# A third pair with fourteen products in the first mixer, and weight sums made by accumulating transfers

## The chip, the cores and the metric

The kernel runs on one core of a Trainium2 chip. The metric is the device time of one execution in microseconds (us). The engines are named as the profile names them: PE multiplies matrices (PEld is its loading of weights, which overlaps it), DVE works element by element on vectors, ACT applies functions and copies, POOL is a general engine that also issues transfers of its own, SP issues most transfers. DMA is the 16 engines that move the data.

## The reference, cut to what matters

A trunk of two residual layers over 256 tokens of 2048 features, all in float32. Layer 0 has stick-breaking attention, layer 1 an attention over selected keys; each is followed by an MLP. The change touches the input projection of layer 0 alone: 256 tokens times a weight of 2048 x 6144.

```python
def stick_breaking_mixer(h, w_in, w_out):
    q, k, v = jnp.split(h @ w_in, 3, axis=-1)      # w_in: 2048 x 6144
    ...                                            # 16 heads of 128
    z = jnp.einsum('bqhd,bkhd->bhqk', q, k) * scale
    log_1mb = jnp.where(causal, jax.nn.log_sigmoid(-z), 0.0)
    tail = lax.cumsum(log_1mb, axis=3, reverse=True) - log_1mb
    a = jnp.where(causal, jnp.exp(jax.nn.log_sigmoid(z) + tail), 0.0)
    ...
    return o @ w_out

x = x + stick_breaking_mixer(rms_norm(x, norm_mix[0]), w_in_a[0], w_out_a[0])
```

## The kernel before

**Items.** The whole kernel is one list of *items*. An item is one block of weights, 256 input features by 512 output columns (512 KB), and the matmuls that use it. A block is loaded into one of six raw tiles (`wraw`, issued by SP), and *split* into two parts whose sum it is: ACT writes the rounded part `wh` (line 2023), DVE the rest `wl` (line 2024). Activations are kept split in the same way. A plain item makes 12 matmuls of 128 x 512: two halves of the tokens, two blocks of 128 features, and for each the parts `wh` with both parts of the activations and `wl` with one. There are four buffers each of `wh` and `wl`, so the split of an item waits for the matmuls of the item four before it.

**Order.** The list is written out by hand, and each engine runs its instructions in the order of the program. For item i the program first issues the split of item i+2 (`LEAD` is 2) and the loads some items further on, then the matmuls of i, and then the steps that are hung on i (`at(i, f)`): steps of the projection first, in the order in which they were hung there, then those of the attention. An instruction that waits holds up all behind it on its engine.

**The first mixer's input projection.** q0, k0 and v0 (512 columns each) are done as 24 plain items (0 to 23). Then come pairs of column groups with the group v1 in between: the first pair (q1 k1, from item 24), v1 (46 to 53), the second pair (q2 k2, from 54), the third pair (q3 k3, from 76) and the fourth (v2 v3). After that comes the output projection.

**Products.** In a pair, some of the work on two column blocks (G and H) is done by a scheme of Strassen's kind: two blocks of 256 features, two halves of the tokens and two column blocks would be eight block products; the scheme needs seven, s1 to s7, of 6 matmuls each, at the price of sums of activations (`sums`, made once) and of weights. A *set* covers two of the eight blocks of features; SEVEN says which: set a the blocks 0 and 2, set b 1 and 3. ROLES gives the order of a pair's items and after which of them its steps stand. The role "mixer" has one set: 12 plain items and 7 products, 19 items. The role "mixer2" has two sets: 8 plain items and 14 products, 22 items. Products of the same name in both sets are summed in PSUM.

**Weight sums.** The sums of weights are the sources of four of the products, which have no block of their own. X feeds s5, Z feeds s6 and later, changed in place, s4, and Y feeds s7. Y is loaded with a block of its own. The steps T1 to T4 make the sums, all on DVE, from the raw tiles of s1, s2 and s3. P1 (ACT), P6, P5 and P7 (DVE) gather the products in E, and `gather` adds the plain items' results.

**Attention in between.** The attention of two heads at a time runs between the items. STEPS gives for each pair of heads the items after which its nine steps stand: logits z (PE, then ACT's copy and abs), exp and ln (ACT), plus (DVE, then POOL's causal select of e, line 1515), sph (ACT), spl (DVE), the tails (PE), the a-step (DVE, then ACT's exp and POOL's select of a), the output (PE, ACT) and its low part (DVE).

**Elsewhere.** The pairs of the MLP and of the output projections follow a planner (`Plan`) and have sums of additions alone; in them T3 is an accumulating transfer from POOL's queue (line 980): it adds a block from DRAM onto a tile.

Of the kernel before, what the change touches and what calls it, by code (L numbers as in the profile page):

```python
# [13 lines left out]
OP = mybir.AluOpType  # L14
# [3 lines left out]
P = 128  # L18
# [33 lines left out]
INNER = {"a": (0, 1), "b": (2, 3)}  # L52
STEPS = ((37, 42, 42, 44, 45, 48, 50, 59, 59),
# [7 lines left out]
ATTENTION = ([("PE", 1.3), ("A", 1.5)], [("A", 1.5)], [("V", 0.9)], [("A", 0.75)], [("V", 0.85)],  # L61
             [("PE", 1.2)], [("V", 0.9), ("A", 0.75)], [("PE", 1.3), ("A", 0.55)], [("V", 0.6)])
ORDER_B = "s1a s1b s5a . . s5b s6a s6b . s7a s7b . s3a s3b s2a s4a s2b s4b G0 G1 G2 G3"
OUT_SUMS = (118, 119)
BIAS = 262
ROLES = {
    "mixer": ("G0 H0 s1 G1 s3 H1 G2 s6 H2 s5 G3 s7 H3 s2 G4 H4 s4 G5 H5", dict(
        T1a=1, T2a=3, T3a=5, T4a=11, P1=5, P6=7, P5=10, P7=11)),
    "mixer2": ("G0 H0 s1a s1b s3a s5a G1 H1 s6a s3b s5b G2 s6b s2b s2a H2 s4a s4b s7a s7b G3 H3", dict(
        T1a=1, T2a=4, T3a=5, T4a=13, T1b=3, T2b=8, T3b=11, T4b=13, P1=3, P6=12, P5=17, P7=19)),  # L70
}


# [278 lines left out]
def trunk(ctx, tc, x, x_t, gains_t, w_in_a, w_out_a, w_in_b, w_in_b_end, w_out_b, rel_bias, w_up, w_down, out):  # L352
# [12 lines left out]
    act, dve, pool, pe = nc.scalar, nc.vector, nc.gpsimd, nc.tensor  # L365
# [3 lines left out]
    keep = tc.keep_in_program_order  # L369
# [30 lines left out]
    room = tmp.tile([P, 2 * P], F32, name="junk", bufs=1)  # L400
# [194 lines left out]
    def block_of(w, r0, c0):  # L595
        return w[r0 // (KB * P), c0 // 512].rearrange("p (a c) -> p a c", a=KB)
# [75 lines left out]
    def sums(at, where, src, s, a, b, n=0):  # L672

        st = {}

        def whole():
            h = src()
            st["a"] = a().rearrange("p q (j s) -> p q j s", j=KB)
            hi, lo = (h[:, 0:4 * KB, i, :].rearrange("p (q j) s -> p q j s", q=2)[
                :, :, KB * n:KB * n + KB] for i in range(2))  # L680
            keep(dve.tensor_add(st["a"], hi.bitcast(F32), lo.bitcast(F32)))

        def four():
            a = st["a"]
            st["b"] = b()
            z = st["b"].rearrange("p (s j) e -> p s j e", s=4)
            (a11, a21), (a12, a22) = ((a[:, q, :, :P], a[:, q, :, P:]) for q in range(2))
            keep(dve.tensor_add(z[:, 0], a21, a22))
            keep(dve.tensor_sub(z[:, 1], z[:, 0], a11))
            keep(dve.tensor_sub(z[:, 2], a11, a21))  # L690
            keep(dve.tensor_sub(z[:, 3], a12, z[:, 1]))

        def high():
            keep(act.activation(s()[:, 0], st["b"], AF.Copy))

        def low():
            keep(dve.tensor_sub(s()[:, 1], st["b"], s()[:, 0].bitcast(F32)))

        for i, step in zip(where, (whole, four, high, low)):
            at(i, step)  # L700

    def seven_products(items, at, sec, w, r0, cols, left, role, S, last=False):
# [34 lines left out]
        products = {}  # L737
# [22 lines left out]
        def own(q, t):  # L760
            return lambda part, j: left()[:, KB * q + j, part, t * P:(t + 1) * P]

        def block(col, q):
            return block_of(w, r0 + KB * P * q, cols[col])

        def spot(pos):
            return base + pos

        def p1():
            keep(act.activation(sec["E"][:, 0], products["s1"], AF.Copy))  # L770

        def p6():
            keep(dve.tensor_add(sec["E"][:, 1], products["s6"], sec["E"][:, 0]))

        def p5():
            keep(dve.tensor_add(sec["E"][:, 2], products["s5"], sec["E"][:, 1]))

        def p7():
            E = sec["E"].rearrange("p (a b) e -> p a b e", a=2)
            keep(dve.tensor_add(E[:, :, 1],  # L780
                                products["s7"].unsqueeze(1).to_broadcast([P, 2, 512]),
                                sec["E"][:, 1:3]))

        def gather(col):
            E = sec["E"][:, 2 * col:2 * col + 2]
            keep(dve.tensor_add(E, accs.pop(keys[col]), E))
# [3 lines left out]
        def one_set(n):  # L790
            qa, qb = SEVEN[n]
            room = sec[n]

            def summed(i):
                return lambda part, j: S(n)[:, part, KB * i + j, :]

            def raw(name):
                return seven[name + n].raw

            def load_y():  # L800
                keep(nc.sync.dma_start(room["Y"], block(1, qa)))

            def t1():
                room["X"] = room["new X"]()
                keep(dve.tensor_sub(room["X"], room["Y"], raw("s1")))

            def t2():
                keep(dve.tensor_sub(room["Z"], raw("s3"), room["X"]))

            def t3():  # L810
                keep(dve.tensor_sub(room["Y"], raw("s3"), room["Y"]))

            def t4():
                keep(dve.tensor_sub(room["Z"], raw("s2"), room["Z"]))

            for name, lhs, src, *to in (
                    ("s1", own(qa, 0), block(0, qa)), ("s2", own(qb, 0), block(0, qb), (0, 0)),
                    ("s3", summed(3), block(1, qb), (1, 0)), ("s4", own(qb, 1), "Z", (0, 1)),
                    ("s5", summed(0), "X"), ("s6", summed(1), "Z"), ("s7", summed(2), "Y")):
                seven[name + n] = seventh(name + n, lhs, src, *to)  # L820
            items[max(base - 8, room.get("read", 0) + 1)].early.append(load_y)
            room["read"] = base + order.index("s7" + n) - LEAD
            for name, step in (("T1", t1), ("T2", t2), ("T3", t3), ("T4", t4)):
                at(spot(place[name + n]), step)
# [283 lines left out]
    class Pair:  # L1108
# [21 lines left out]
        def block(self, col, q):  # L1130
            return block_of(self.w, self.r0 + KB * P * q, self.cols[col])
# [261 lines left out]
    def mixer_a():  # L1393
# [3 lines left out]
        sec = {"a": {}, "b": {}}  # L1397
# [178 lines left out]
        def out_rooms(heads):  # L1576
# [21 lines left out]
            for hp, where in enumerate(STEPS):  # L1598
                for i, work in zip(where, ATTENTION):
                    weave.plan.busy[i] += work  # L1600
            weave.out_columns(
                w_out_a, lambda: heads, parts, lambda i: st["oT", i], dict(zip("ab", OUT_SUMS)), {},
                {"aX": STEPS[7][0], "aZ": STEPS[7][0], "bX": STEPS[7][7], "bZ": STEPS[7][7]}, ORDER, 32)
# [3 lines left out]
            group(*front[g], q)  # L1607
        for g in range(FRONT):
            single(*front[g], FRONT * (QB - 1) + g)
        roles = ["mixer2", "mixer2", "mixer", "mixer"]  # L1610
        for names in "q1 k1,v1,q2 k2,q3 k3,v2 v3".split(","):
            groups = [(name[0], int(name[1])) for name in names.split()]
            if len(groups) == 2:
# [368 lines left out]


    sections = [mixer_a(), mlp(0, 16), mixer_b(), mlp(1, None)]
    items = [it for sec in sections for it in sec[0]]
    first, sizes, plans = {}, {}, {}
# [134 lines left out]
```

## Time and profile before

| | |
|---|---|
| time, median of 3 runs | 1988.82 us (1988.48 to 1989.84) |
| span of the profiled execution (first to last instruction) | 1986.8 us |
| PE busy | 1980.4 us, 8834 matmuls |
| DVE busy | 1785.0 us |
| ACT busy | 1301.7 us |
| POOL busy | 91.7 us |
| DMA | 498.44 MB, of which 33.56 MB by accumulating transfers |

The profiled execution has no time of its own beside its span; its time is taken as the span and the 2.0 us by which the median of the runs is above it. Busy time is the time in which an engine has an instruction under way; for PE it includes a wait inside the pipeline, which shows as a greater distance between matmuls. In the timelines a row is a start, a duration, an engine, a line of the kernel, an operation, what it writes and reads, and a count; engines overlap the end of one instruction with the start of the next, so the distance of two starts is a little less than the duration.

### The profile page before, as it was taken

The page shows a single profiled execution, that of the slowest core. Times are in us where ns is not written, and L with a number is a line of the kernel's source. Part 1 is how long each engine was busy: PE and PEld are TensorE (multiplying, and loading weights), DVE is VectorE, ACT ScalarE, POOL GpSimd, SP SyncE. Part 2 cuts the span into 40 slices and gives each one's busy share as a digit, 9 for nine tenths or more (in the row PEclk, how much of TensorE's full clock was granted, in tenths as well). Part 3 has the DMA queues.
Part 4 walks back from the last instruction along what each step waited for, and adds up shares of the span by engine and source line. Part 5 has one row for each costly group of instructions (what it writes and reads, how often), then busy time and mean ns, then how long its engine had stood idle before and what let it go on. Part 6 is the DMA issues. An engine that isn't in the chain of part 4 may idle for free.

```text
span 1986.8 us, 25525 instructions
## 1 busy us (share of the span) xinstructions
PE 1980.4 (100%) x8834; PEld 1635.3 (82%) x8834; DVE 1785.0 (90%) x1973; ACT 1301.7 (66%) x1573; POOL 91.7 (5%) x135
## 2 busy tenths in 40 slices
PE   9999999999999999999999999999999999999999
PEld 7888888888888888888888788788888888888887
DVE  6879869899999999989995898889998998998996
ACT  6567666667676676766764566666767676776664
POOL 0000100000000000020000000000000000000000
PEclk9999999999999999999999999999999999999999
DMA  9776766889788977889887698578887888788784
GB/s 350 215 238 189 218 211 181 275 289 292 244 259 257 278 235 239 288 277 295 247 291 235 190 264 255 153 264 281 290 265 244 254 269 271 224 286 276 256 244 146
DMA packets 233441, 498.44 MB, mean 251 GB/s; under 512 B 88608, under 2 KB 121440, under 8 KB 233312
## 3 DMA queue, kind: packets, MB, share of 16 engines
q1 hardware_dynamic: 216048, 455.81, 68.8%
q0 software_dynamic: 9216, 33.56, 9.4%
q10 hardware_dynamic: 8048, 7.45, 1.1%
q8 instruction: 69, 1.13, 0.2%
q14 instruction: 60, 0.49, 0.1%
HBM read 459.46 MB, written 37.22 MB: 250 GB/s over the span
## 4 chain that ended last, share of the span: by engine, by line
PE 99%; DVE 0%; DMA 0%; issue 0%; ACT 0%; SPq 0%; DVEq 0%
PE acc L1169 39%; PE acc L1151 26%; PE acc L628 17%; PE acc L732 5%; PE aux L1151 4%; PE aux L751 2%; PE acc L751 1%; PE acc L619 1%; PE aux L1851 0%; PE acc L1494 0%; PE aux L1554 0%; PE acc L1739 0%; PE aux L1169 0%; PE acc L1704 0%; PE aux L1556 0%; PE acc L1496 0%
## 5 line engine op out<-in xcount | busy, mean ns | idle before, releaser
L2024 DVE TENSOR_TENSOR wl<-wraw,wh 128x1024 fp32r<-128x1024 f32 (+1 forms) x670 | 805.5, 1217 | 134.6 <-ACT wh L2023 121.9
L2023 ACT ACTIVATE wh<-wraw 128x1024 fp32r<-128x1024 f32 (+1 forms) x670 | 700.0, 1053 | 317.8 <-PE acc L1169 110.7
L1169 PE MATMUL acc<-wh,xT 128*128 128x512 f32 x1152 | 284.6, 389 | 0.0
L1169 PEld LDWEIGHTS acc<-wh,xT 128*128 128x128 f32 x1152 | 216.2, 188 | 45.2 <-ACT wh L2023 0.3
L1169 PE MATMUL acc<-wh,half 128*128 128x512 f32 x1004 | 248.2, 389 | 0.0
L1169 PEld LDWEIGHTS acc<-wh,half 128*128 128x128 f32 x1004 | 188.5, 188 | 39.1
L1151 PE MATMUL acc<-wh,half 128*128 128x512 f32 x720 | 192.4, 389 | 0.0
L628 PE MATMUL acc<-wh,xT 128*128 128x512 f32 x736 | 185.5, 392 | 0.0
L628 PEld LDWEIGHTS acc<-wh,xT 128*128 128x128 f32 x736 | 137.6, 188 | 30.0 <-issue 1.7
L1151 PEld LDWEIGHTS acc<-wh,half 128*128 128x128 f32 x720 | 135.2, 188 | 28.1
L1169 PE MATMUL acc<-wl,xT 128*128 128x512 f32 x576 | 154.0, 389 | 0.0
L1169 PE MATMUL acc<-wl,half 128*128 128x512 f32 x502 | 134.4, 389 | 0.0
L1169 PEld LDWEIGHTS acc<-wl,xT 128*128 128x128 f32 x576 | 108.1, 188 | 22.5
L1151 PE MATMUL acc<-wl,half 128*128 128x512 f32 x360 | 110.8, 389 | 0.0
L1169 PEld LDWEIGHTS acc<-wl,half 128*128 128x128 f32 x502 | 94.2, 188 | 19.5
L628 PE MATMUL acc<-wl,xT 128*128 128x512 f32 x368 | 99.2, 391 | 0.0
L2023 ACT ACTIVATE wh<-Zb 128x1024 fp32r<-128x1024 f32 x60 | 63.5, 1058 | 41.5 <-PE acc L1169 14.4
L1151 PE MATMUL acc<-wh,xT 128*128 128x512 f32 x336 | 89.8, 389 | 0.0
L628 PEld LDWEIGHTS acc<-wl,xT 128*128 128x128 f32 x368 | 68.9, 188 | 15.0 <-DVE wl L2024 0.3
L732 PE MATMUL acc<-wh,xT 128*128 128x512 f32 x320 | 79.7, 391 | 0.0
L1151 PEld LDWEIGHTS acc<-wl,half 128*128 128x128 f32 x360 | 67.6, 188 | 14.0
L2024 DVE TENSOR_TENSOR wl<-Za,wh 128x1024 fp32r<-128x1024 f32 x60 | 73.4, 1223 | 0.7 <-ACT wh L2023 0.6
(404 smaller groups left out, 3087.2 us busy)
## 6 DMA issues: line engine op xcount, KB each, us to landing
wraw<-in_w_up_dram SPq DMA_DIRECT2D x228, 512.0 KB, 5.4
wraw<-in_w_down_dram SPq DMA_DIRECT2D x224, 512.0 KB, 5.1
wraw<-in_w_in_a_dram SPq DMA_DIRECT2D x88, 512.0 KB, 4.9
wraw<-in_w_in_b_dram SPq DMA_DIRECT2D x64, 512.0 KB, 4.8
jx<-tu SPq DMA_DIRECT2D x44, 512.0 KB, 5.8
tu<-y SPq DMA_DIRECT2D x128, 128.0 KB, 3.6
wraw<-in_w_out_a_dram SPq DMA_DIRECT2D x30, 512.0 KB, 3.6
wraw<-in_w_out_b_dram SPq DMA_DIRECT2D x30, 512.0 KB, 4.4
```

Source lines behind the costliest of these rows:

```text
L619: pin(pe.matmul(accs[key][t], L[:, j, part, t * P:(t + 1) * P], wx[:, j, :], start=(j == 0 and n == 0), stop=False))
L628: (keep if alone else pin)(pe.matmul(acc[t], L[:, KB * q + j, part, t * P:(t + 1) * P], wx[:, j, :], start=a and q == 0, stop=z and q == Q ...
L732: keep(pe.matmul(acc[:, t, :], L[:, KB * qs[i] + j, part, t * P:(t + 1) * P], wx[:, j, :], start=a and i == 0, stop=z and i == end - (last ...
L751: keep(pe.matmul(p, lhs(part, j), wx[:, j, :], start=to is None and a and n == sets[0], stop=to is None and z and n == sets[-1]))
L1151: keep(pe.matmul(o, lhs(part, j), wx[:, j, :], start=a and opens, stop=z, skip_group_check=True))
L1169: keep(pe.matmul(acc[:, t, :], L[:, KB * q + j, part, t * P:(t + 1) * P], wx[:, j, :], start=a and i == 0 and not self.sets, stop=z, skip_ ...
L2023: order(act.activation(wh[:, a], raw[:, a], AF.Copy))
L2024: order(dve.tensor_sub(wl[:, a], raw[:, a], wh[:, a].bitcast(F32)))
```

## The change

The third pair takes the role "mixer2" instead of "mixer": two sets, 22 items instead of 19. Everything after it in the mixer stands three items later (STEPS, OUT_SUMS), and the steps of the attention that fall into the third pair are moved a little against its items. T3 and T4 become accumulating transfers issued from POOL's queue, in all four pairs; since a transfer can only add, the signs of the sums of activations, of T1 and T2 and of the gathering steps are turned so that all sums of weights are additions. T3 and T4 stand earlier in the pair (T3a after its third item instead of the sixth, T4a after the ninth instead of the 14th or 12th). P7 becomes two instructions of half the size.

```diff
-         (59, 61, 61, 65, 66, 79, 85, 97, 105),
-         (67, 73, 75, 79, 86, 89, 90, 107, 113),
-         (87, 88, 88, 90, 91, 104, 105, 117, 117),
-         (92, 95, 97, 103, 106, 109, 110, 121, 121),
+         (59, 61, 61, 65, 66, 80, 86, 100, 108),
+         (67, 73, 75, 80, 88, 91, 93, 110, 116),
+         (89, 90, 90, 93, 95, 107, 108, 120, 120),
+         (95, 98, 100, 106, 109, 112, 113, 124, 124),
...
-OUT_SUMS = (118, 119)
+OUT_SUMS = (121, 122)
...
     "mixer": ("G0 H0 s1 G1 s3 H1 G2 s6 H2 s5 G3 s7 H3 s2 G4 H4 s4 G5 H5", dict(
-        T1a=1, T2a=3, T3a=5, T4a=11, P1=5, P6=7, P5=10, P7=11)),
+        T1a=1, T2a=3, T3a=2, T4a=8, P1=5, P6=7, P5=10, P7=11)),
     "mixer2": ("G0 H0 s1a s1b s3a s5a G1 H1 s6a s3b s5b G2 s6b s2b s2a H2 s4a s4b s7a s7b G3 H3", dict(
-        T1a=1, T2a=4, T3a=5, T4a=13, T1b=3, T2b=8, T3b=11, T4b=13, P1=3, P6=12, P5=17, P7=19)),
+        T1a=1, T2a=4, T3a=2, T4a=8, T1b=3, T2b=8, T3b=4, T4b=11, P1=3, P6=12, P5=17, P7=19)),
...
-            keep(dve.tensor_add(z[:, 0], a21, a22))
+            keep(dve.tensor_sub(z[:, 0], a21, a22))
             keep(dve.tensor_sub(z[:, 1], z[:, 0], a11))
             keep(dve.tensor_sub(z[:, 2], a11, a21))
-            keep(dve.tensor_sub(z[:, 3], a12, z[:, 1]))
+            keep(dve.tensor_add(z[:, 3], a12, z[:, 1]))
...
         def p5():
-            keep(dve.tensor_add(sec["E"][:, 2], products["s5"], sec["E"][:, 1]))
+            keep(dve.tensor_sub(sec["E"][:, 2], products["s5"], sec["E"][:, 1]))
 
         def p7():
-            E = sec["E"].rearrange("p (a b) e -> p a b e", a=2)
-            keep(dve.tensor_add(E[:, :, 1],
-                                products["s7"].unsqueeze(1).to_broadcast([P, 2, 512]),
-                                sec["E"][:, 1:3]))
+            E = sec["E"]
+            keep(dve.tensor_sub(E[:, 3], E[:, 2], products["s7"]))
+            keep(dve.tensor_add(E[:, 1], products["s7"], E[:, 1]))
...
             def t1():
                 room["X"] = room["new X"]()
-                keep(dve.tensor_sub(room["X"], room["Y"], raw("s1")))
+                keep(dve.tensor_add(room["X"], room["Y"], raw("s1")))
 
             def t2():
-                keep(dve.tensor_sub(room["Z"], raw("s3"), room["X"]))
+                keep(dve.tensor_add(room["Z"], raw("s3"), room["X"]))
 
             def t3():
-                keep(dve.tensor_sub(room["Y"], raw("s3"), room["Y"]))
+                keep(pool.dma_start(room["Y"], block(1, qb), accum_op=OP.add))
 
             def t4():
-                keep(dve.tensor_sub(room["Z"], raw("s2"), room["Z"]))
+                keep(pool.dma_start(room["Z"], block(0, qb), accum_op=OP.add))
...
-        roles = ["mixer2", "mixer2", "mixer", "mixer"]
+        roles = ["mixer2", "mixer2", "mixer2", "mixer"]
```

4 rows, old and new, of the table STEPS are left out of this document.

## The prediction

> **What bounds the kernel now.** I read the head of the page, the chain that ended last, and then a table of stretches cut where the pairs of the first mixer's input projection begin (71.01, 137.25, 184.34 and 231.14 us; the third pair is the stretch from 184.34).
>
> ```profile
> span 1986.8 us, 25525 instructions
> PE 1980.4 (100%) x8834; PEld 1635.3 (82%) x8834; DVE 1785.0 (90%) x1973; ACT 1301.7 (66%) x1573; POOL 91.7 (5%) x135
> ...
> PE 99%; DVE 0%; DMA 0%; issue 0%; ACT 0%; SPq 0%; DVEq 0%
> ```
>
> ```profile
> core 0: us, PE busy (x) PEld busy (x) DVE busy (x) ACT busy (x) POOL busy (x), PEclk, DMA share, GB/s
> 71.01:114.40 43.39, 43.39 (x198) 36.11 (x196) 40.26 (x37) 28.73 (x32) 1.69 (x2) 1.00 0.72 222
> ...
> 137.25:184.34 47.09, 47.09 (x220) 39.47 (x218) 42.51 (x40) 33.58 (x40) 3.46 (x4) 1.00 0.61 208
> 184.34:231.14 46.80, 46.80 (x216) 39.03 (x214) 38.26 (x36) 28.55 (x34) 5.97 (x8) 1.00 0.72 218
> ```
>
> The chain is 99% PE, and in every pair PE is busy for the whole stretch at clock 1.00. So a matmul less is worth its full time, an operation of another engine taken away is worth nothing, and any new wait of PE is lost whole: nothing later catches it up. DVE is nearly as full (40.26 of 43.39, 42.51 of 47.09, 38.26 of 46.80 us), so its queue is where a new wait would come from.
>
> The profiled execution's span is 1986.8 us against a median of 1988.82 us, so 2.0 us lie around the span. I make the sum as a difference and put it on 1988.82.
>
> **The change, part by part.**
>
> *Products.* The next fence has PE's timeline in the third pair: start, us, engine, line, operation, count. A line of several matmuls is one item or half of one.
>
> ```profile
> 212.37 2.10 PE L732 MATMUL acc<-wh,xT 128*128 128x512 f32 x8
> ...
> 216.58 0.39 PE L1530 MATMUL acc<-sph,tri 128*128 128x512 f32 x1
> ...
> 217.51 2.00 PE L732 MATMUL acc<-wh,xT 128*128 128x512 f32 x8
> ...
> 220.26 1.98 PE L732 MATMUL acc<-wh,xT 128*128 128x512 f32 x8
> ...
> 222.98 1.07 PE L751 MATMUL acc<-wh,xT 128*128 128x512 f32 x4
> ...
> 224.34 0.59 PE L1494 MATMUL acc<-qk 128*128 128x256 f32 x2
> ...
> 225.56 2.10 PE L732 MATMUL acc<-wh,xT 128*128 128x512 f32 x8
> ```
>
> A plain item (12 matmuls) takes 222.98-220.26 = 2.72 us, a product (6) 224.34-222.98 = 1.36 us: 0.2267 us a matmul. The logits of a pair of heads take 225.56-224.34 = 1.22, the tails 217.51-216.58 = 0.93. The third pair goes from 12 plain items and 7 products (186 matmuls) to 8 and 14 (180): 6 x 0.2267 = **1.36 us less**.
>
> *Splits and sums on DVE and ACT.* Three more items are three more splits on ACT and on DVE. Sums on DVE fall from 24 (six sets of four) to 14 (seven of two), 10 x 1.14 us; P7 becomes two halves in each pair. Over the mixer DVE gets lighter; PE hides it before and after, so I cost all of it at nothing, except where the order makes PE wait. In the third pair alone DVE does not get lighter: two sums a set, two sets, makes four as before, with three splits more (3 x 1.14 us) in a stretch 1.36 us shorter.
>
> *The new wait, at the third pair's G3.* In the new order the four products s4a, s4b, s7a, s7b (items 92 to 95) stand in a row, and G3 is item 96. The new STEPS put the logits of heads 8 and 9 after item 89, their exp, ln and plus at 90, the tails of heads 6 and 7 after 91, and the a-step of heads 6 and 7 and sph of heads 8 and 9 at 93. The split of item i+2 is issued ahead of item i's matmuls, so G3's split stands on ACT behind that exp of a and sph; they stand behind the a-step on DVE, and that behind the splits of 93, 94 and 95 and P5. The rows that price this, ACT first, then DVE:
>
> ```profile
> 212.65 0.81 ACT L1499 ACTIVATE z<-acc 128x768 f32<-128x768 f32 x1 [2.87 <-PE acc L1496]
> 213.49 0.85 ACT L1500 ACTIVATE e<-z 128x768 f32<-128x768 f32 x1
> 214.24 1.05 ACT L2023 ACTIVATE wh<-wraw 128x1024 fp32r<-128x1024 f32 x1
> 215.19 0.83 ACT L1504 ACTIVATE e<-e 128x768 f32<-128x768 f32 x1
> 216.05 0.85 ACT L1505 ACTIVATE e<-e 128x768 f32<-128x768 f32 x1
> 216.80 1.04 ACT L2023 ACTIVATE wh<-wraw 128x1024 fp32r<-128x1024 f32 x1
> ...
> 221.34 0.85 ACT L1542 ACTIVATE a<-a 128x768 f32<-128x768 f32 x1 [2.55 <-DVE a L1540]
> 222.10 0.83 ACT L1520 ACTIVATE sph<-e 128x768 fp32r<-128x768 f32 x1
> 222.83 1.99 ACT L2023 ACTIVATE wh<-wraw 128x1024 fp32r<-128x1024 f32 x2
> ```
>
> ```profile
> 210.01 0.68 DVE L776 TENSOR_TENSOR oTc<-aux,oTc 128x512 f32<-128x512 f32 x1
> 210.61 0.95 DVE L1524 TENSOR_TENSOR spl<-e,sph 128x768 fp32r<-128x768 f32 x1
> ...
> 216.93 0.96 DVE L1509 SCALAR_TENSOR_TENSOR e<-z,e 128x768 f32<-128x768 f32 x1 [0.39 <-ACT e L1505]
> 217.88 1.23 DVE L2024 TENSOR_TENSOR wl<-wraw,wh 128x1024 fp32r<-128x1024 f32 x1
> 219.02 1.43 DVE L2024 TENSOR_TENSOR wl<-oTc,wh 128x1024 fp32r<-128x1024 f32 x1
> 220.37 0.94 DVE L1540 TENSOR_TENSOR a<-z,acc 128x768 f32<-128x768 f32 x1
> ```
>
> Let T be the end of the logits after item 89. PE then has s2a 1.36, H2 2.72, the tails 0.93, four products 5.44 and the next logits 1.22: it comes to G3 at T+11.67. ACT: z's copy at T+0.28 (212.65-212.37), abs 0.84 later, split 92 0.75 later, exp 0.95 later, ln 0.86 later at T+3.68; ln ends at T+4.53, and split 93 may start at T+4.43. DVE: plus at T+4.56 (0.03 after ln, as at 216.93), free again 0.95 later, T+5.51. Three splits of 1.14 (219.02-217.88) reach T+8.93, P5 (0.60) T+9.53, the a-step ends 0.94 later at T+10.47. ACT: exp of a at T+10.50, sph 0.76 later, G3's split 0.73 later at T+11.99, done 1.04 later at T+13.03. PE waits 13.03-11.67 = **1.36 us**. What keeps this hidden now is that only two products stand between the plain items there. Its ends: 0 (if DVE is two splits earlier than laid out) and 2.0 (if P5 or the plus comes half a microsecond later). I take 1.36. Elsewhere the same laying out leaves 0.3 us or more.
>
> *The accumulating transfers.* T3 and T4 of all seven sets go to POOL's queue: 14 more, of 512 KB. The rows of those that stand in the kernel already: the queue's share, issue to landing by target, all together, and one group's time on POOL.
>
> ```profile
> q0 software_dynamic: 9216, 33.56, 9.4%
> ```
>
> ```profile
> qk<-in_w_out_a_dram POOLq DMA_DIRECT2D x1, 512.0 KB, 8.8
> Yb<-in_w_out_a_dram POOLq DMA_DIRECT2D x1, 512.0 KB, 8.0
> ```
>
> ```profile
> L980 POOL DMA_DIRECT2D Ya<-in_w_up_dram x14: 862/862/888, 403.1 to 1764.5; - x14
> ...
> DMA to landing us min/median/max: 5.5/8.6/10.8
> ```
>
> T3 has 7 items or more until its sum is split, and T4 of set a has 6, 8 us at the least of the items' own time: I cost both at nothing, covered by the products and plain items between. T4b has least: issued after item 11 of the pair, its sum split for item 17. It waits for DVE's split of s6b, and in the third pair also for the select of heads 4 and 5 (item 86), which stands ahead of it in POOL's queue.
>
> ```profile
> 207.95 0.77 POOL L1515 TENSOR_SCALAR_AFFINE_SELECT a<-a 128x256 f32<-128x256 f32 x2 [21.03 <-ACT a L1542]
> ...
> 218.02 2.69 POOL L1515 TENSOR_SCALAR_AFFINE_SELECT e<-e 128x256 f32<-128x256 f32 x2 [9.30 <-DVE e L1509]
> ```
>
> ```profile
> 161.93 1.21 DVE L2024 TENSOR_TENSOR wl<-vsb,wh 128x1024 fp32r<-128x1024 f32 x1
> ```
>
> ```profile
> 163.97 1.07 PE L751 MATMUL aux<-wh,oTb 128*128 128x512 f32 x4
> ```
>
> In the second pair that split ends (163.14) 0.83 us before its item starts (163.97). With T3a's sum (1.14) gone from DVE's queue I take 2.0 before. Then a-step 0.94, exp 0.88, select 0.77: T4b is issued 0.6 us after s6b starts, and since s6b, s2b and the logits take 3.94 us, at T-3.3. Its sum is wanted at T+4.43, so there are 7.7 us, and what the landing takes beyond that adds to the chain above one for one. Ends: 5.5 us, nothing; 10.8 us, 3.1. I take 8.0, the row of the same room in the same mixer: **0.3 us**. In the first two pairs no a-step, exp and select stand ahead, 2.6 us, so there are some 10 us and only landings past 10 cost there: 0.8 each at 10.8.
>
> The Trainium skill, "DMA: Bandwidth & Descriptors", section on the anatomy of a transfer issued by GpSimd, fits its time as 2.0 us plus the bytes over 436 GB/s, by my estimate 3.2 us for 512 KB; with it this term would be 0 and the sum 1988.8. The rows above (5.5 at least) do not agree.
>
> *DMA load.* 9.4% of 1986.8 us over 64 transfers is 2.92 us of all 16 engines each. The third pair has 0.72 x 46.80 = 33.7 us now; with four more, 45.4 of 45.4 us. The weight loads land in 4.4 us (the next row is of that stretch), and six raw tiles let them be issued several items ahead, so I cost this at nothing; but it is why an accumulate may land late. SP's queue gets no more transfers: 15 blocks and one Y become 14 and two.
>
> ```profile
> wraw<-in_w_in_a_dram SPq DMA_DIRECT2D x15, 512.0 KB, 4.4
> ```
>
> *Sum:* -1.36 + 1.36 + 0.3 = +0.3: **1989.1 us**.
>
> **The rivals.**
>
> 1. *All hidden.* G3 comes in time, T4b too: 1988.82-1.36 = 1987.5. For it: PE waits nowhere in the pairs now. Against: the chain above, which is short only if DVE runs over a microsecond earlier.
>
> 2. *T4b held at POOL.* The select ahead of it takes 2.69 instead of 0.77 us, as the selects of e do beside DVE: T4b 1.9 later, 2.2 us late in all, 1988.82-1.36+1.36+2.2 = 1991.0. Against: the row of the select of a. (The Trainium skill, "SBUF — State Buffer", section "Who interferes with whom", says that a DVE instruction with two SBUF inputs contends with a GpSimd instruction that reads SBUF, which speaks against the change; the two rows agree in kind, without saying which select is hit.)
>
> 3. *Slower: accumulates late from full DMA engines.* Place: the split of s4b, worst in the third pair. At 10.8 us it costs 3.1 there and 0.8 in each of the first two pairs: 1988.82-1.36+1.36+4.7 = 1993.5. It passes 0.2% at a landing of 10.6 us, where 2.9 and twice 0.6 make 4.1. For it: the share of 1.0 worked out above, where the MLP's landings were measured with two accumulates in a pair and not four. Against: the two in the output projection landed in 8.0 and 8.8.
>
> **How the numbers follow.** Forecast (PE loses about what it saves, 1988.3 to 1990.0): 0.50. All hidden: 0.25. Held at POOL or landing 9 to 10 us: 0.14. Late by full engines: 0.10, eight tenths of it past 0.2%. Something else: 0.01. 0.2% is 4.0 us, about what a measurement of this kernel tells from no change. Faster by more: 0.01, as only 1.36 us are there to gain; slower by more: 0.08; within: 0.91. Range 1987.2 to 1992.2: it holds the forecast, all hidden with the spread of the runs, and rival 2. The forecast's own is 1988.3 to 1990.0.
>
> **What would show it.** PE has 8828 matmuls, six fewer. PE shows a gap of 1 to 2 us just ahead of G3 of the third pair, with ACT's wh as what ended it, and exp of a and sph just before that split on ACT. If rival 1 holds there is no gap, and the span falls by 1.4. If T4b is late, ACT's split of Z for s4b is ended by the transfer, and the landing reads 9 us or more. DVE loses about 8 us of busy time in the mixer, and DMA's share in the third pair goes to 0.9 or more. The prediction is wrong if weight loads end ACT's or DVE's waits there for microseconds, or if PE waits in the first two pairs.

## The result, and the profile after

The changed kernel takes **2001.03 us** (median of 5 runs, 1999.38 to 2004.55) against 1988.82 us (1988.38 to 1989.84): a ratio of 1.0061, 95% interval 1.0049 to 1.0073. It is 12 us slower, where 1989.1 us was forecast and 1992.2 us was the end of the range. The page of the changed kernel:

```profile
span 1999.3 us, 25563 instructions
...
PE 1983.6 (99%) x8828; PEld 1634.8 (82%) x8828; DVE 1779.2 (89%) x1970; ACT 1305.5 (65%) x1576; POOL 103.1 (5%) x149
...
q0 software_dynamic: 11232, 40.90, 11.3%
...
PE 94%; DVE 2%; DMA 1%; issue 1%; ACT 1%; SPq 0%; DVEq 0%; ACTq 0%
```

PE has the 8828 matmuls that were forecast, but the chain is 94% PE instead of 99%, with DVE, DMA, ACT and "issue" in it. The profiled run is the median one (1999.3 of span, 2001.03 in all), so its trace tells where the 12.5 us of span went. The stretches, from 0.3 us ahead of where each pair's matmuls begin: first, second, third and fourth pair, with the same columns as in the prediction.

```profile
70.81:114.41 43.60, 43.60 (x197) 35.91 (x196) 35.28 (x33) 27.95 (x32) 5.25 (x6) 1.00 0.92 261
137.27:186.30 49.03, 47.68 (x220) 39.30 (x219) 36.82 (x35) 32.32 (x37) 6.86 (x8) 1.00 0.79 242
186.30:242.26 55.96, 48.91 (x211) 38.88 (x209) 40.79 (x39) 31.43 (x36) 9.42 (x12) 0.97 0.79 218
242.26:291.74 49.48, 48.52 (x221) 40.03 (x222) 39.20 (x37) 32.01 (x39) 5.89 (x8) 1.00 0.79 230
```

Before, cut in the same way, the fourth pair reads

```profile
230.83:278.90 48.07, 48.07 (x224) 40.23 (x223) 39.01 (x37) 30.87 (x37) 4.15 (x6) 1.00 0.71 213
```

Against before the second pair is 1.9 us longer (49.03 - 47.09), the third 9.2 (55.96 - 46.80) and the fourth 1.4 (49.48 - 48.07); the first, 0.2. The third pair has 1.36 us of matmuls less, so it loses 10.5 us. Its mean granted clock is 0.97, not 1.00. PE's waits, as engine, line, releaser, us in total, times, longest:

```profile
PE acc L1493 <- DMA qk<-td: 4.5, 1, 4.5
PE acc L751 <- ACT wh L2022: 2.7, 2, 1.4
PE acc L732 <- ACT wh L2022: 1.4, 2, 0.8
...
PE acc L732 <- DVE wl L2023: 0.6, 1, 0.6
```

None of these four groups is there before. The largest is one wait in the third pair, and it isn't for an accumulating transfer at all: PE stands at the logits of heads 8 and 9 for `qk`, the turned k2. q2 and k2 are written by SP in four pieces each to a DRAM tile `td` and read back into `qk`. SP's rows (start, us in issue, count) before, then after, each with the time from the read's issue to its landing:

```profile
194.82 4.07 SPq L461 DMA_DIRECT2D td<-jx  x4
...
201.38 0.33 SPq L466 DMA_DIRECT2D qk<-td  x1
```

```profile
DMA to landing us min/median/max: 5.0/5.0/5.0
```

```profile
197.05 10.07 SPq L461 DMA_DIRECT2D td<-jx  x4
...
211.79 0.33 SPq L466 DMA_DIRECT2D qk<-td  x1
```

```profile
DMA to landing us min/median/max: 8.5/8.5/8.5
```

Before, k2 landed at 206.4 and PE took it at 211.14 (line 1494): 4.8 us early. After, the writes begin 2.2 us later (2.0 of them are the later start of the whole pair, which PE shares), take SP 10.07 us instead of 4.07, and the read takes 3.5 us longer, so k2 lands at 220.3. PE stood there from 216.0 (220.43 less 4.46, below). What follows on PE:

```profile
213.97 1.20 PE L751 MATMUL acc<-wh,xT 128*128 128x512 f32 x4 [1.39 <-ACT wh L2022]
...
220.43 0.84 PE L1493 MATMUL acc<-qk 128*128 128x256 f32 x2 [4.46 <-DMA qk<-td]
...
222.63 1.90 PE L751 MATMUL acc<-wh,xT 128*128 128x512 f32 x4
...
224.82 2.01 PE L732 MATMUL acc<-wh,xT 128*128 128x512 f32 x8
...
236.23 2.11 PE L732 MATMUL acc<-wh,xT 128*128 128x512 f32 x8 [0.78 <-ACT wh L2022]
```

Four matmuls take 1.90 us at 222.63 where they took 1.07 before: after the long wait PE ran at half rate (the granted clock reads 0.50 from 221 to 224 us). The logits take 222.63-220.43 = 2.20 instead of 1.22 us and the product 2.19 instead of 1.36, 1.8 us more. The first row is another new wait, s2b's split, and ACT's row gives its cause, a block of weights from SP. The last is the forecast wait of G3.

```profile
212.86 1.06 ACT L2022 ACTIVATE wh<-wraw 128x1024 fp32r<-128x1024 f32 x1 [1.31 <-DMA wraw<-in_w_in_a_dram]
```

The time in brackets is idle time, counted from the modelled end of the matmul before. Undisturbed, a matmul starts before that end, and after a wait the next ones stand further apart, so a wait costs some 0.3 to 0.6 us more than its bracket (the section on the prediction works this out for G3). Counted from start to start against the undisturbed lengths, 10.4 of the 10.5 us of the third pair are placed: 1.9 at s2b's block, 4.7 at the logits, 1.8 of half rate, 1.2 at G3 and 0.8 at the fourth pair's first item (G0, bracket 0.61).

In the second pair the late one is T4b, whose sum s4b takes: its transfer was issued at 163.83 and landed 11.6 us later.

```profile
175.49 1.06 ACT L2022 ACTIVATE wh<-vsb 128x1024 fp32r<-128x1024 f32 x1 [2.22 <-DMA vsb<-in_w_in_a_dram]
...
176.60 1.20 PE L751 MATMUL acc<-wh,xT 128*128 128x512 f32 x4 [1.29 <-ACT wh L2022]
```

From start to start this one wait costs the 1.9 us that the second pair is longer.

And the share of the DMA engines, in slices of 5 us, before and then after:

```profile
190.00:195.00 5.00, 5.00 (x25) 4.23 (x24) 4.91 (x6) 3.88 (x5) 0.00 (x0) 1.00 1.00 233
195.00:200.00 5.00, 5.00 (x23) 4.13 (x22) 4.92 (x5) 3.44 (x4) 0.00 (x0) 1.00 1.03 252
200.00:205.00 5.00, 5.00 (x23) 4.13 (x22) 3.57 (x5) 2.12 (x2) 0.00 (x0) 1.00 0.91 274
205.00:210.00 5.00, 5.00 (x23) 4.13 (x22) 3.14 (x4) 2.74 (x3) 0.77 (x2) 1.00 1.02 419
210.00:215.00 5.00, 5.00 (x26) 4.21 (x25) 4.96 (x6) 2.32 (x3) 0.00 (x0) 1.00 0.47 165
```

```profile
200.00:205.00 5.00, 5.00 (x24) 4.13 (x23) 4.93 (x5) 3.35 (x4) 1.17 (x2) 1.00 1.10 261
205.00:210.00 5.00, 5.00 (x24) 4.14 (x23) 4.92 (x6) 1.62 (x2) 0.19 (x1) 1.00 1.14 187
210.00:215.00 5.00, 3.61 (x16) 2.48 (x14) 1.73 (x2) 2.80 (x3) 1.59 (x3) 1.00 1.04 392
215.00:220.00 5.00, 0.91 (x3) 0.30 (x2) 4.00 (x5) 1.23 (x2) 0.00 (x0) 1.00 1.05 288
```

The mean of 0.72 over the third pair before hid four slices at 0.91 to 1.03: from 190 to 210 us the engines were already full, at 233 to 274 GB/s for the most part, while the turned q2 and k2 were written and read back. The stretch had no room where the first three accumulating transfers of the third pair are issued (194.9, 199.6 and 204.3 us); the fourth, at 212.3, falls where the engines of before stood at 0.47 and those of after are still full.

### The profile page after: what moved, and what is told of

It is laid out like the page before. It is cut to its first block, busy times and chain, and to the rows that moved or that the text cites. A ratio compares the mean times of both kernels' runs of the same rounds, so it can differ in the third digit from the quotient of the medians.

```text
span 1999.3 us, 25563 instructions
## 1 busy us (share of the span) xinstructions
PE 1983.6 (99%) x8828; PEld 1634.8 (82%) x8828; DVE 1779.2 (89%) x1970; ACT 1305.5 (65%) x1576; POOL 103.1 (5%) x149
## 3 DMA queue, kind: packets, MB, share of 16 engines
q0 software_dynamic: 11232, 40.90, 11.3%
## 4 chain that ended last, share of the span: by engine, by line
PE 94%; DVE 2%; DMA 1%; issue 1%; ACT 1%; SPq 0%; DVEq 0%; ACTq 0%
PE acc L1168 39%; PE acc L1150 26%; PE acc L628 17%; PE aux L1150 4%; PE acc L732 3%; PE aux L751 1%; ACT wh L2022 1%; PE acc L751 1%; PE acc L619 1%; DMA vsb<-in_w_in_a_dram 1%; DVE wl L2023 1%; PE aux L1850 0%; DMA qk<-td 0%; DMA td<-jx 0%; PE acc L1738 0%
## 5 line engine op out<-in xcount | busy, mean ns | idle before, releaser
L2023 DVE TENSOR_TENSOR wl<-wraw,wh 128x1024 fp32r<-128x1024 f32 (+2 forms) x669 | 802.9, 1214 | 143.7 <-ACT wh L2022 136.6
L2022 ACT ACTIVATE wh<-wraw 128x1024 fp32r<-128x1024 f32 (+2 forms) x669 | 699.8, 1054 | 330.9 <-PE acc L1168 116.5
L1168 PE MATMUL acc<-wh,xT 128*128 128x512 f32 x1152 | 284.5, 389 | 0.0
L1168 PEld LDWEIGHTS acc<-wh,xT 128*128 128x128 f32 x1152 | 216.2, 188 | 44.9
L628 PE MATMUL acc<-wh,xT 128*128 128x512 f32 x736 | 185.6, 392 | 0.0
L628 PEld LDWEIGHTS acc<-wh,xT 128*128 128x128 f32 x736 | 137.5, 188 | 30.4 <-issue 1.7
L1150 PE MATMUL acc<-wh,xT 128*128 128x512 f32 x336 | 89.8, 389 | 0.0
L1150 PEld LDWEIGHTS acc<-wh,xT 128*128 128x128 f32 x336 | 63.1, 188 | 13.1
```

Of the source, the lines that this page charges most:

```text
L628: (keep if alone else pin)(pe.matmul(acc[t], L[:, KB * q + j, part, t * P:(t + 1) * P], wx[:, j, :], start=a and q == 0, stop=z and q == Q ...
L1150: keep(pe.matmul(o, lhs(part, j), wx[:, j, :], start=a and opens, stop=z, skip_group_check=True))
L1168: keep(pe.matmul(acc[:, t, :], L[:, KB * q + j, part, t * P:(t + 1) * P], wx[:, j, :], start=a and i == 0 and not self.sets, stop=z, skip_ ...
L2022: order(act.activation(wh[:, a], raw[:, a], AF.Copy))
L2023: order(dve.tensor_sub(wl[:, a], raw[:, a], wh[:, a].bitcast(F32)))
```

## The experiments

The theory after this reading, **A**: the 12 us are two costs. One is DMA: accumulating transfers meet the turn of q2 and k2 and the weight blocks on full engines, and what is late then is the turned k2 (and, less, T4b and a weight block). The other is the order in the third pair, with four products in a row, and in the fourth: splits stand behind the attention's steps on ACT and DVE. The rival **B** changes its form from one group of runs to the next: first, that the fourteen products in the third pair cost it by themselves; then, that the sums gone from DVE's queue and the issues on POOL do it whatever the bytes.

**Each half alone.** `sums_alone` has T3 and T4 by transfer, but roles, STEPS and OUT_SUMS of before.

```diff
-        roles = ["mixer2", "mixer2", "mixer2", "mixer"]
+        roles = ["mixer2", "mixer2", "mixer", "mixer"]
```

> The accumulating transfers (T3 and T4 of every set, with the turned signs) without the second set in the third pair: the third pair keeps 12 plain items and 7 products, the attention its old places. Theory A, the 14 transfers fill the DMA engines, and what waits for a transfer (Z for s4b, the turned q2 and k2) is what PE waits for: 8834 matmuls, waits of about 0.3 us at s4b of the first pair and 1.5 us at s4b of the second remain as in the changed kernel, the third pair's turned k2 comes 2 x 2.9 us later than before, against some 5 us that it had over, so 0 to 2 us there: 1990.5 to 1993. Theory B, the third pair's new order alone makes the loss of 12 us and the transfers matter only at s4b: 1990.5 to 1991.0, nothing lost after the second pair.

Measured: 1996.21 us, ratio 1.0037 (1.0024 to 1.0051): above what both expected. Its one large wait, and the slice in which it ends (at 217.44), with the granted clock in the third column from the right:

```profile
PE acc L1493 <- DMA qk<-td: 5.1, 1, 5.1
```

```profile
215.00:220.00 5.00, 2.56 (x9) 2.24 (x9) 0.15 (x1) 0.00 (x0) 0.00 (x0) 0.50 1.03 419
```

Only the sums went from DVE to transfers, and the wait for k2 is there whole, with the clock at 0.50 in its last part and behind it.

`pair_alone` is the other half: the second set in the third pair with the changed STEPS, and T3 and T4 on DVE in every pair, at the places of before.

```diff
-                keep(pool.dma_start(room["Y"], block(1, qb), accum_op=OP.add))
+                keep(dve.tensor_add(room["Y"], room["Y"], raw("s3")))
...
-                keep(pool.dma_start(room["Z"], block(0, qb), accum_op=OP.add))
+                keep(dve.tensor_add(room["Z"], room["Z"], raw("s2")))
```

> The second set in the third pair with the changed kernel's order and attention places, but T3 and T4 of every set are DVE additions at their old places in the pair (with the turned signs, so all additions). Theory A: no added transfers, so the read of the turned k2 lands by 210 us, as before, and the 4.5 us wait of the logits of heads 8 and 9 is gone, and with it the half-rate matmuls behind it; what is left is the queue of DVE and ACT ahead of G3 of the third pair, 1 to 3 us with the four sums on DVE: 1988.5 to 1990.5. Theory B (the order of the third pair itself is the cause): 1996 or more, with waits of over 3 us in the third pair.

Measured: 1994.55 us, ratio 1.0028 (1.0017 to 1.0039): between the two. No wait for a transfer, but five on ACT and DVE, of 0.5 to 1.0 us, between 220 and 251 us, and one of 0.2 at 210. Both halves cost, 7.3 and 5.7 us over the 1988.9 us of before beside them. That their sum, 13.0, is near the 12.2 of the change is chance: 3.4 of the 5.7 come from T3 and T4 on DVE, where the changed kernel doesn't have them (1994.55 - 1991.11, `eighth_bytes` below).

`third_on_dve` takes the changed kernel and puts only the third pair's sums back on DVE (the role "mixer2_dve" there).

> The changed kernel, but T3 and T4 of the third pair's two sets are DVE additions at the old places of the role; the other three pairs keep the transfers. Theory A: the waits in the first two pairs stay (0.5 and 1.7 us), those in the third pair fall to the 1 to 3 us of DVE's and ACT's queue, the fourth pair loses about 1 us: 1990.5 to 1993.5. Theory B (it is the order, wherever the sums are made): 1998 or more.

Measured: 1996.09 us, ratio 1.0038 (1.0025 to 1.005): again between. It showed the transfers' share only in part, since the sums on DVE bring back the waits of `pair_alone`. The wait for k2 is gone.

**The wait itself.** `logits_late` is the changed kernel with the logits of heads 8 and 9 five items later, and those of heads 10 and 11 behind them:

```diff
-         (89, 90, 90, 93, 95, 107, 108, 120, 120),
-         (95, 98, 100, 106, 109, 112, 113, 124, 124),
+         (94, 95, 95, 97, 98, 107, 108, 120, 120),
+         (100, 102, 104, 107, 109, 112, 113, 124, 124),
```

> The changed kernel, but the logits of heads 8 and 9 stand after item 94 instead of 89 with exp, ln and plus after 95, sph 97, spl 98, and the logits of heads 10 and 11 after item 100 with exp and ln 102, plus 104, sph 107; nothing else moves. Theory A: the turned k2 that landed at 220.3 us is then wanted about 8 us later, so the 4.5 us wait and the matmuls at half rate behind it go, some 6 us, while the late Z for s4b of the third pair (landed 221.4) may now be waited for, 0 to 3 us: 1995 to 1998. A rival, that the third pair is behind on weight blocks as such and PE loses the time at the next block instead: 2000 or more.

Measured: 1994.55 us, ratio 1.003 (1.0019 to 1.004): 6.5 us come back, a little more than A expected; the rival's 2000 falls. PE doesn't wait for k2 at all (it landed at 220.3, the logits start at 226.61). The trace has one wait for a turned tile, 0.6 us at 269.35, but that is k3, for the logits of heads 12 and 13. The engines are as full as in the changed kernel (0.99 and 1.04 in the slices from 210 to 220), and now s2b's weight block is late by more, 2.47 instead of 1.39 us, with half rate behind it (1.85 us for four matmuls):

```profile
213.29 1.85 PE L751 MATMUL acc<-wh,xT 128*128 128x512 f32 x4 [2.47 <-ACT wh L2022]
```

**The bytes.** `eighth_bytes` keeps every instruction, place and wait of the changed kernel and takes seven eighths of the bytes away, so that its sums of weights are incomplete.

```diff
-                keep(pool.dma_start(room["Y"], block(1, qb), accum_op=OP.add))
+                keep(pool.dma_start(room["Y"][:, :1, :128], block(1, qb)[:, :1, :128], accum_op=OP.add))
```

(T4 likewise.)

> The changed kernel with every instruction, place and wait kept, but each T3 and T4 transfer adds only 128 of a partition's 1024 columns (64 KB instead of 512 KB), so the sums of weights are incomplete: the time is that of the order without the bytes. Theory A (the bytes keep the 16 DMA engines full when the turned q2 and k2 are written and read): the wait of the logits of heads 8 and 9 for the read of k2 goes (4.5 us before), and so do the half-rate matmuls behind it and the waits for T4b; what is left is ACT and DVE's order, 0.8 at the third pair's G3 and about 1.3 in the fourth pair, against 1.36 us of matmuls saved: 1988.5 to 1991. Theory B (the sums gone from DVE's queue and the issues on POOL set the order, bytes are no matter): 1999 to 2002, wait for k2 over 3 us.

Measured: 1991.11 us, ratio 1.0011 (1.0002 to 1.002); ten of its eleven executions took 1990.48 to 1992.36 us, one 6875.22. That is 0.1 us above A's range and far from B's. Of the 12.2 us some 10 are gone with the bytes alone: B falls. What is left is order only, on PE:

```profile
223.56 0.70 PE L1493 MATMUL acc<-qk 128*128 128x256 f32 x2 [0.19 <-DVE a L1539]
226.11 2.12 PE L732 MATMUL acc<-wh,xT 128*128 128x512 f32 x8 [0.98 <-ACT wh L2022]
232.45 2.11 PE L732 MATMUL acc<-wh,xT 128*128 128x512 f32 x8 [0.59 <-ACT wh L2022]
247.40 1.20 PE L732 MATMUL acc<-wl,xT 128*128 128x512 f32 x4 [0.57 <-DVE wl L2023]
```

They are the logits of heads 10 and 11, G3 of the third pair, and G0 and H1 of the fourth. k2 landed at 208.9, 2.5 us before PE came to its logits.

`plain_copies` moves all the bytes again, but without adding:

```diff
-                keep(pool.dma_start(room["Y"], block(1, qb), accum_op=OP.add))
+                keep(pool.dma_start(room["Y"], block(1, qb)))
```

> The changed kernel with T3 and T4 as plain transfers of the same 512 KB that overwrite the tile instead of adding to it, so the sums are left out. From the queues' rows of the page of before, a plain 512 KB takes 1.57 us of all engines (68.8% of 1986.8 us for 455.81 MB) and an accumulating one 2.92. Theory A by engine time: a little over half the load stays, the wait for k2 falls to 0 to 3 us, 1991 to 1996. If only accumulating as such is the trouble (reading and writing the tile): as with few bytes, 1988.5 to 1991. Theory B: 1999 to 2002.

Measured: 1991.26 us, ratio 1.0012 (1.0003 to 1.0021), no different from an eighth of the bytes. It lies at the low end of A's range (1991 to 1996) and just above that of accumulating as such (1991 at the most), so the time doesn't tell these two apart. Its queue, and its writes and read of k2:

```profile
q0 software_dynamic: 11232, 40.90, 10.3%
```

```profile
194.22 5.87 SPq L461 DMA_DIRECT2D td<-jx  x4
...
204.02 0.33 SPq L466 DMA_DIRECT2D qk<-td  x1
```

```profile
DMA to landing us min/median/max: 7.8/7.8/7.8
```

The same 40.90 MB in the same 11232 packets take 10.3% of 1989.5 us, against 11.3% of 1999.3 us in the changed kernel and 9.4% of 1986.8 us before: 18.2 us for the fourteen plain transfers, 39.2 us for the accumulating ones, so 1.3 and 2.8 us of all engines each (the shares are rounded, which is 0.1 us either way). With the plain ones k2 lands at 204.02 + 7.8 = 211.8 us, and the logits start at 211.92, without a wait in the list and some 0.2 us later than the matmuls before would let them. So k2 came 2.5 us early with few bytes, just in time with plain transfers and 4.5 us late with accumulating ones: what was in hand is used up to the last by the plain form, and what the accumulating form adds on top is paid in full. Why it takes twice the engine time of a plain one isn't shown.

**Where the transfers hurt.** `sums_not_third` is `sums_alone` with the third pair's one T3 and T4 back on DVE.

```diff
-        roles = ["mixer2", "mixer2", "mixer", "mixer"]
+        roles = ["mixer2", "mixer2", "mixer_dve", "mixer"]
```

> Accumulating transfers in the first, second and fourth pair; the third pair is that of before (one set, sums on DVE), STEPS of before. Against the kernel with transfers in all four pairs and the roles of before (1996.21) only two transfers go, those that stand in the stretch where the turned k2 is written. Theory A: no wait for k2, 1989 to 1991 (0.5 for T4b of the second pair, 0 to 1 in the others). Theory B (bytes no matter, the issues in other pairs or a shift of DVE's work before the turn set it): 1994 to 1996.5, as the shift of 1.9 us in the start of the turned k2's write comes from the second pair.

Measured: 1989.74 us, ratio 1.0004 (0.9995 to 1.0013): two transfers of 512 KB were worth 6.5 us, and ten in the other pairs nothing that can be measured (the trace has the second pair 0.9 us longer). A as expected.

`t3_plain` and `t4_plain` exchange one kind only for plain transfers in the changed kernel.

> The changed kernel with T3 as plain transfers that overwrite (sums Y left out), T4 accumulating as changed. Theory A1 (the accumulating T3 of the third pair, issued at 194.9 and 199.6 us as the turned k2 is written, are what pushes it): the wait of the logits of heads 8 and 9 for k2 falls from 4.5 to under 1 us and the half-rate matmuls go; the waits for T4b (1.45 in the second pair, up to 1.2 in the third) stay: 1992 to 1995. Theory A2 (T4 does it, or any accumulating transfer alike): 1996 to 2000, wait for k2 over 2 us.

> The changed kernel with T4 as plain transfers that overwrite (sums Z of s4 left out), T3 accumulating as changed. Theory A1: the wait for k2 stays at 3 to 5 us with the half-rate matmuls behind it, and no s4b waits: 1996 to 2000. Theory A2: 1992 to 1995.

Measured: T3 plain 1995.13 us, ratio 1.0031 (1.002 to 1.0043); T4 plain 1994.2 us, ratio 1.0026 (1.0014 to 1.0037), with runs from 1992.41 to 1998.47. Neither A1 nor A2 as written (A2's time fits with T4 plain, not with T3 plain): 5.9 and 6.8 us come back for the one and the other, and 9.8 for both. The wait for k2 is 1.9 us in the first and 4.3 in the profiled run of the second, which was the slowest of its seven. Neither kind alone is the cause; either one taken away returns more than half. With T4 plain two executions of the same program differ by up to 6 us, where the kernel before has 1.7: what is late by how much differs from one execution to the next. Which wait varies isn't shown, since one execution of each kernel has a trace.

**The order.** `pair_eased` has no transfers and moves the attention's steps in the third pair: the later logits of `logits_late`, the a-step of heads 4 and 5 two items earlier, T4a of the third pair one earlier.

```diff
-         (59, 61, 61, 65, 66, 80, 86, 100, 108),
+         (59, 61, 61, 65, 66, 80, 84, 100, 108),
```

> No accumulating transfers in the mixer; the second set in the third pair, with the attention's steps eased: the a-step of heads 4 and 5 two items earlier, the logits of heads 8 and 9 after item 94 and of heads 10 and 11 after 100, and T4 of set a an item earlier. Theory A (the 5.6 us lost by the third pair without transfers are DVE's queue from 210 to 226 us, overfilled by the attention's steps placed there, so that each step moved out gives PE its wait back): 1987.5 to 1991. Theory C (DVE has too much work in the third pair with two sets whatever the order): 1993 to 1996 as with the steps unmoved (1994.55).

Measured: 1992.03 us, ratio 1.0015 (1.0006 to 1.0024): 2.5 us back, between A and C. The earlier a-step made a new wait at G2, and half rate from five matmuls later on (1.91 us for four matmuls):

```profile
208.78 2.74 PE L739 MATMUL acc<-wh,xT 128*128 128x512 f32 x8 [1.87 <-ACT wh L2035]
211.31 1.91 PE L739 MATMUL acc<-wl,xT 128*128 128x512 f32 x4
```

`pair_eased2` puts that step back after item 86; `pair_eased3` also has the logits of heads 8 and 9 one item later, after 95.

> The eased order without accumulating transfers in the mixer (1992.03), with the a-step of heads 4 and 5 back after item 86: there PE waited 1.87 us for G2's split behind that a-step's exp, and ran eight matmuls at half rate after it, 1.6 us. Theory A (order alone): both go, and of the 5.6 us that the third pair lost without transfers some 0.5 to 1.5 stays: 1987.8 to 1990. Theory C (DVE has too much to do in the third pair): the wait turns up elsewhere, 1991 to 1993.

> As the one before, with the logits of heads 8 and 9 one item later (after 95), so that they needn't wait for the bank that the a-step of heads 6 and 7 frees (0.3 to 0.5 us). Theory A: 0 to 0.5 us less than the one before, 1987.5 to 1990. Theory C: 1991 to 1993.

Measured: 1992.47 us, ratio 1.0016 (1.0007 to 1.0025), and 1991.22 us, ratio 1.0011 (1.0002 to 1.002). In the first of the two G2's wait is gone, and waits of 0.60 and 1.17 us for DVE's wl and of 1.07 for the a-step stand in its place. In the second DVE is busy for 9.93 of 10 us while PE loses over one:

```profile
215.00:225.00 10.00, 8.82 (x41) 7.04 (x40) 9.93 (x11) 4.02 (x4) 0.00 (x0) 1.00 0.70 224
```

The same stretch of `eighth_bytes`, with the sums off DVE:

```profile
215.00:225.00 10.00, 9.81 (x47) 7.95 (x45) 7.56 (x7) 6.42 (x8) 3.24 (x4) 1.00 0.39 123
```

So theory C holds for that stretch: with two sets of sums DVE is full there, and a step moved out only brings the wait to another place. No kernel tried here is faster than the one before. Whether another order of the products would be was not tried; only 1.36 us are there to gain.

| kernel | T3, T4 | third pair | median, us |
|---|---|---|---|
| before | DVE | one set | 1988.82 |
| `sums_not_third` | transfers, but not in the third pair | one set | 1989.74 |
| `sums_alone` | transfers | one set | 1996.21 |
| `eighth_bytes` | transfers of 64 KB | two sets | 1991.11 |
| `plain_copies` | plain transfers | two sets | 1991.26 |
| `pair_alone` | DVE | two sets | 1994.55 |
| changed | transfers | two sets | 2001.03 |

## Why the prediction was wrong, step by step

- **"DMA load ... I cost this at nothing": the step that failed**, by about 10 us (2001.03 - 1991.11). The engine time was right: 2.92 us a transfer was estimated and 2.8 measured. The load was right too: it was laid out at 45.4 us of a stretch of 45.4, and 0.79 of 55.96 us is 44.2 (so the share itself stayed below the 0.9 that was to show it). The error was to find the engines full and to ask only whether weight blocks and the accumulates themselves would be late. The turned q2 and k2 were in none of the rows that I read, though they share the same 16 engines, and the 5 us slices of the trace of before show those full from 190 to 210 us. "SP's queue gets no more transfers" was true and beside the point: the transfers that it had took longer.
- **Rival 3 had the resource and not the victim.** It put the price on the split of s4b (1993.5). s4b was late once, in the second pair, where the landing took 11.6 us and PE waited 1.29; by the prediction's own price, what the landing takes beyond some 10 us, that is 1.6. The third pair's wait was 4.46 us for k2, 1.8 us of half rate behind it, and 1.39 for a weight block. The prediction's own list of what would make it wrong had the weight blocks and the waits in the second pair, and not k2.
- **The new wait at G3, 1.36 us: right in mechanism, and near in size.** The bracket reads 0.98 us with few bytes and 0.78 in the changed kernel, but the prediction counted from start to start. So counted, in `eighth_bytes`, G3 begins 1.21 us late (at 226.11, where the logits before it would have let it begin at 224.90), and its item takes 2.87 instead of 2.72 us: 1.36 in all. With T at 212.60, DVE's plus stands where it was laid out (217.17); G3's split begins 0.4 us later than laid out and PE comes to G3 0.6 later, which nearly cancels. In the changed kernel ACT's order is as laid out: exp of a at 233.65, sph at 234.40, G3's split at 235.14. That this term and the matmuls saved come to the same 1.36 us is chance.
- **"Elsewhere the same laying out leaves 0.3 us or more": wrong three times**, at the logits of heads 10 and 11 (bracket 0.19, for the a-step of heads 6 and 7) and at G0 (0.59) and H1 (0.57) of the fourth pair. G0's wait comes over ACT: abs of heads 10 and 11 waits for DVE's spl of heads 8 and 9, which frees the tile e, and G0's split stands behind it.

```profile
230.61 0.85 ACT L1499 ACTIVATE e<-z 128x768 f32<-128x768 f32 x1 [2.91 <-DVE spl L1523]
231.36 1.99 ACT L2022 ACTIVATE wh<-wraw 128x1024 fp32r<-128x1024 f32 x2
```

  From start to start they cost 0.47, 0.88 and 0.88 us (the logits 0.36 late and 0.11 slower, the other two 0.75 late and 0.13 slower). With them the sum without the bytes is 1988.82 - 1.36 + 1.36 + 0.47 + 0.88 + 0.88 = 1991.05 us; `eighth_bytes` measured 1991.11.
- **T4b, 0.3 us.** In the third pair it stood behind the select, as laid out (select at 211.63 for 0.77 us, T4b at 212.34), and landed in 9.0 us, which the prediction prices at 1.3 us; nobody waited, since PE was by then late itself. Rival 2 didn't come about.
- **The splits and sums at nothing:** right for the first two pairs. DVE's busy time fell by 5.8 us, where 8 were forecast. Left on DVE, T3 and T4 would have cost more than nothing: `pair_alone` against `eighth_bytes`, the same order of items, is 3.4 us.
- **All hidden (0.25)** fell on both costs. That a wait of some microseconds is followed by half rate, 1.8 us here, was in no term.

## What to carry to other kernels

Read the DMA share in slices as short as the slack that you rely on, and for every stretch at 1.0 list all that is in flight there with its slack to its user: the first victim of a new transfer need not be the transfer itself. An accumulating transfer took about twice the engine time of a plain one of the same bytes; count that, and not bytes. Where PE is the bound, count a wait from start to start: the short ones here cost 0.3 to 0.6 us more than their bracket, and those of 1.87 us and more also 1.7 to 2.2 us of half rate.

## What the runs showed of the hardware

- **Half rate after a wait.** Six traces have a wait of PE of 1.87 us or more in the third pair (5.13, 4.46, 4.28, 2.47, 1.89 and 1.87 us), and in each the granted clock goes to 0.50, where matmuls of 512 columns start some 427 ns apart instead of 227. After waits of 1.39, 1.29 and 0.98 us the clock stayed at 1.00. In slices of 1 us it reads 0.90, 0.50, 0.50, 0.50 and 0.90 from 220 to 225 us in the changed kernel, so 3.4 us in all. It was 3.4 us too after the waits of 2.47, 1.89 and 1.87; after the last it began only five matmuls behind the wait. In `sums_alone` (5.13) it reads 0.86, six times 0.50 and 0.73 from 214 to 222: 6.8 us, of which 2.7 were still wait, and likewise after the 4.28 of `t4_plain`. The matmuls behind the six waits took 1.7 to 2.2 us longer than undisturbed (2.2 in `sums_alone`: the logits 2.55 instead of 1.22, the item after them 3.57 instead of 2.72). The Trainium skill, "TensorE: Matmul & The Clock Gate", section "Part 1: The HAM clock gate (the "warmup" mystery)", has the clock halved after an idle window of about 3.4 us and back after about 3.4 us of work. The second half of that agrees, with 3.4 to 4.2 us at half rate once PE had work; the first doesn't, as a wait of 1.87 us was enough here.
- **Transfers issued from POOL.** The fourteen accumulating transfers of the first mixer's pairs landed in 5.8 to 11.6 us (T4, the next row) and the plain ones at the same places in 3.5 at the least (T3, the row after). The Trainium skill, "DMA: Bandwidth & Descriptors", section "Anatomy of one DMA — SWDGE (gpsimd) path" (GpSimd is POOL here), has 2.0 us plus the bytes over 436 GB/s, by my estimate 3.2 us for 512 KB. That is near the best of the plain ones, and far from all of the accumulating ones.

```profile
DMA to landing us min/median/max: 5.8/9.0/11.6
```

```profile
DMA to landing us min/median/max: 3.5/6.3/9.1
```
